# A depthwise convolution of the context tokens reads its taps from PSUM instead of from a padded copy in SBUF

## The chip, the cores and the metric

The kernel runs as one program on one core of a Trainium2 chip. Its time is the device time of one execution in microseconds, and the median over the runs is what counts. Besides that there is one profiled execution, whose instructions are all recorded; the rows below are from it. The engines are named as the profile names them: PE is TensorE (PEld its weight loads), DVE VectorE, ACT ScalarE, POOL GpSimd, and SP issues most DMAs.

## The reference, cut to what matters

One layer of a hybrid backbone: 512 latent tokens and 256 context tokens of 1024 channels. The context goes through the same input projection as the latents; its channels are convolved along the tokens, and only the final state of a scan over them is kept, as the start of the latent scans. Everything else (the latents' own convolution and scan, pooling, the output projection, a mixture of 32 experts) follows.

```python
def dwconv_centred(u, w, b):                       # 5 taps, 2 to each side, zeros beyond the ends
    y = lax.conv_general_dilated(u, w[:, None, :].astype(u.dtype), window_strides=(1,),
        padding=[(SSD_CONV // 2, SSD_CONV // 2)],
        dimension_numbers=("NWC", "WIO", "NWC"), feature_group_count=ch)
    return y + b.astype(u.dtype)
...
pc = hc @ w_in[l][:, :(XBCDT_COLS if last else IN_COLS)]
xbc_c = jax.nn.silu(dwconv_centred(pc[..., :CONV_CH], conv_w[l], conv_b[l]))
...
init_states = (ssd_final_state(xbc_c, dt_c, dt_bias[l], a_log[l], 0),
               ssd_final_state(xbc_c, dt_c, dt_bias[l], a_log[l], 1))
```

## The kernel before, in words

All data is fp32. A product is made of three matmuls of rounded halves: ACT writes the high part `hi` of a weight piece (L228), DVE or POOL the rest `lo` (L231), and PE multiplies hi by the high and low halves of the activations and lo by the high half.

The stage that the change touches is the loop over four head groups g at the end of the context's work. In each turn it issues, as written:

- for g = 0, 1 and 3 a block of the gate's projection (`z_block`, L353 to L355 on PE, ended by L369 on ACT and L370 on DVE);
- `ctx_conv(g)`: the group's four column blocks of 128 channels, two at a time (two halves, below called a and b). PE transposes them to channels on partitions (L447, into a PSUM bank of tag `S`, four such banks), ACT copies the bank to `xp` in SBUF (L452) between two zeroed columns on each side (POOL, L450 and L451), DVE applies the first tap and the bias (L456) and the other four taps (L459), each over all 256 tokens, ACT takes the tanh (L462), DVE completes the SiLU (L389), PE transposes back (L467), and ACT copies the result to `xc` (L468);
- `ctx_proj(g + 1)`: the next group's projection;
- `mod_row(g)`: one row of 1024 modulation values as a matrix-vector product outside PE: eight pieces of 512 KB are loaded into `mraw` (three buffers, L417 on SP's queue), the even ones are scaled by ACT (L419) and summed by POOL (L421), the odd ones are multiplied and summed by DVE (L423, L425), POOL adds both sums (L426), PE adds over the partitions (L432), DVE adds the bias (L434, for one row also L437), and the row is stored (L438, on ACT's queue) out of two more `mraw` buffers;
- `ctx_state(g)`: POOL scales `xc` (L407), PE makes the two states (L409), ACT copies them out (L477).

After the last group the memory of this stage is released, and the latents' groups start: their projections (`project`, L336 to L338) have their convolution taken straight from PSUM by `taps` (ACT L374 for the middle tap and the bias, DVE L378 for the four others). The first five of these projections (120 matmuls) need no memory of the context stage up to their convolution, so they run inside it.

A scheduler sets the order on each engine from its own estimate of the times: the program is written group by group, and it interleaves whatever it expects to be ready. The order is fixed when the program is built; on the chip each engine takes its list strictly in turn and waits on semaphores. SP's list is such a queue too: a load whose buffer isn't free holds up the loads behind it.

Of the kernel before, what the change touches and what calls it, by code (L numbers as in the profile page):

```python
# [5 lines left out]
F32 = mybir.dt.float32  # L6
# [4 lines left out]
AF = mybir.ActivationFunctionType  # L11
ALU = mybir.AluOpType
# [4 lines left out]
P = 128  # L17
# [3 lines left out]
TC = 256  # L21
# [76 lines left out]
def mixer_and_moe(tc, a):  # L98
    nc = tc.nc
    SC, VE, PO, PE, SP = nc.scalar, nc.vector, nc.gpsimd, nc.tensor, nc.sync  # L100
# [22 lines left out]
    def bank(tag):  # L123
        return psa.tile([P, T], F32, name="A", tag="A", bufs=4) if tag == "A" else \
            psb.tile([P, T], F32, name=tag, tag=tag, bufs=BUFS[tag])
# [83 lines left out]
    cw = pk.tile([P, 5, 20], F32, name="cw")  # L209
    cb = pk.tile([P, 20], F32, name="cb")  # L210
# [25 lines left out]
    for k in range(KT):  # L236
        for h in range(2):
# [7 lines left out]
            with tc.issue_after(wdma.ins):  # L245
                if 2 * k + h in (5, 9):
                    j = k // 2 - 1
# [41 lines left out]
    for j in range(16):  # L289
# [8 lines left out]
                            op0=ALU.add, op1=ALU.mult)  # L298
# [11 lines left out]
    for lo, n, which, oh_, ol_ in ((NT, NTC, 1, hch, hcl), (0, NT, 0, hxh, hxl)):  # L310
        for k in range(KT):
            tp = bank("S")
            w = n * P
            for j in range(n):
# [3 lines left out]
                             op0=ALU.mult, op1=ALU.add)  # L318
# [6 lines left out]
    pa = tc.alloc_tile_pool(name="pctx", bufs=1, side="left", reuse_waits="tile")  # L325
# [47 lines left out]
    def taps(ac, src, ct, n):  # L373
        SC.activation(ac, src, AF.Identity, scale=cw[:, 2, ct:ct + 1], bias=cb[:, ct:ct + 1])  # L374
        for j in (0, 1, 3, 4):
            o = j - 2
            u, v = max(0, -o), n - max(0, o)
            VE.scalar_tensor_tensor(ac[:, u:v], src[:, u + o:v + o], cw[:, j, ct:ct + 1], ac[:, u:v],  # L378
                                    op0=ALU.mult, op1=ALU.add)
# [8 lines left out]
    def silu_to(out, ac, tt):  # L388
        VE.scalar_tensor_tensor(out, tt, 1.0, ac, op0=ALU.add, op1=ALU.mult)  # L389
# [50 lines left out]
    def ctx_conv(g, ctxp):  # L440
        xc = pa.tile([P, NTC, T], F32, name="xc", bufs=2)
        for j2 in range(2):
            tp = bank("S")
            for i in range(2):
                j = 2 * j2 + i
                for c in range(NTC):
                    PE.transpose(tp[:, i * TC + c * P:i * TC + (c + 1) * P], ctxp[:, c, j * P:(j + 1) * P], ident)  # L447
            xp = pa.tile([P, 2, TC + 4], F32, name="xp2", bufs=2)
            ac = pa.tile([P, 2, TC], F32, name="ac2", bufs=2)
            PO.memset(xp[:, :, 0:2], 0.0)  # L450
            PO.memset(xp[:, :, TC + 2:], 0.0)  # L451
            SC.activation(xp[:, :, 2:2 + TC], tp.rearrange("p (i t) -> p i t", i=2), AF.Copy)  # L452
            for i in range(2):
                j = 2 * j2 + i
                ct = g * 3 + j if j < 3 else 12 + g
                VE.tensor_scalar(ac[:, i, :], xp[:, i, 0:TC], cw[:, 0, ct:ct + 1], cb[:, ct:ct + 1],  # L456
                                 op0=ALU.mult, op1=ALU.add)
                for q in range(1, 5):
                    VE.scalar_tensor_tensor(ac[:, i, :], xp[:, i, q:q + TC], cw[:, q, ct:ct + 1], ac[:, i, :],  # L459
                                            op0=ALU.mult, op1=ALU.add)  # L460
            tt = xp[:, :, 0:TC]
            SC.activation(tt, ac, AF.Tanh)  # L462
            silu_to(ac, ac, tt)
            tp = bank("S")
            for i in range(2):
                for c in range(NTC):
                    PE.transpose(tp[:, c * TC + i * P:c * TC + (i + 1) * P], ac[:, i, c * P:(c + 1) * P], ident)  # L467
            SC.activation(xc[:, :, j2 * TC:(j2 + 1) * TC], tp.rearrange("p (c t) -> p c t", c=NTC), AF.Copy)  # L468
        return xc
# [87 lines left out]
    for g in range(G):  # L557
        if g in ZP:
            z_block(ZP.index(g), pa, "tz")
        xcs[g] = ctx_conv(g, ctxps.pop(g))  # L560
        if g + 1 < G:
            ctxps[g + 1] = ctx_proj(g + 1)
        mod_row(g)
        init[g] = ctx_state(g, xcs.pop(g))
# [3 lines left out]
    pa = tc.alloc_tile_pool(name="pa", bufs=1, side="left", reuse_waits="tile")  # L568
# [216 lines left out]
    for i, ts in enumerate(cat):  # L785
        for j in range(3 + i):
            t = pcat.tile([P, 2, 4, 2 * P], F32R, name=f"cat{i}{j}", tag="raw", bufs=RC)
# [18 lines left out]
    for pr in range(2):  # L806
        cath, catl = cat[pr]
        for k2 in range(6):
            tp = bank("S")
# [5 lines left out]
            for i in range(2):  # L815
# [5 lines left out]
                                        op0=ALU.mult, op1=ALU.subtract)  # L821
# [1001 lines left out]
```

## Time and profile before

| | us |
|---|---|
| median of 3 runs | 1787.97 |
| lowest and highest of them | 1785.37 and 1789.52 |
| the profiled execution: device time | 1785.24 |
| its span, first to last instruction | 1783.4 |
| the context stage's conv part, first L447 to last L467 | 102.46 to 262.42 |
| the stream of the experts' weights | from about 480 to the end |

The device time of the profiled execution is 1.8 us longer than its span. In the rows below a time is counted from the span's start; "x4" is the number of instructions merged into a row, and the bracket at the end of a row says how long the engine was idle before it and what ended the idle time.

### The profile page before, as it was taken

How to read it: one execution, taken by the hardware profiler on the slowest of the kernel's cores; microseconds unless marked ns; L12 is line 12 of the kernel's file. 1: busy time of each engine (PE TensorE's matmuls, PEld its weight loads, DVE VectorE, ACT ScalarE, POOL GpSimd, SP SyncE). 2: the span in 40 equal slices, each digit the busy share in tenths (PEclk: the TensorE clock that was granted, in tenths of full speed). 3: DMA queues.
4: the chain of work that ended last, by engine and by line, in shares of the span. 5: the costliest groups of instructions: out<-in, count | busy, mean ns of one | idle time of the engine just before them, and what ended most of it. 6: DMA issues, size and time to landing. Idle time of an engine off the chain costs nothing. (4 is left out here: it accounts for less than half of the span.)

```text
span 1783.4 us, 21256 instructions
## 1 busy us (share of the span) xinstructions
PE 1634.9 (92%) x7311; PEld 1199.5 (67%) x7311; DVE 1524.0 (85%) x1486; ACT 1170.2 (66%) x1207; POOL 594.1 (33%) x287
## 2 busy tenths in 40 slices
PE   6999889998899899999999999999999998999995
PEld 2777667776777777767767667676666666666663
DVE  7767888987876989999989999966899999999994
ACT  6445336556643567787777877755678777787773
POOL 1213456779210102152040541502053454313302
PEclk9999899999999999999999999998999999999998
DMA  9646453323468789999999999985899999999973
GB/s 353 196 132 212 148 159 100 108 78 112 174 233 332 285 333 356 375 392 380 376 375 391 357 382 392 356 309 197 335 381 383 381 369 363 386 387 366 387 262 103
DMA packets 138417, 521.44 MB, mean 292 GB/s; under 512 B 14798, under 2 KB 44942, under 8 KB 106560
## 3 DMA queue, kind: packets, MB, share of 16 engines
q1 hardware_dynamic: 125446, 490.39, 72.4%
q0 software_dynamic: 6736, 16.70, 4.0%
q10 hardware_dynamic: 6122, 12.94, 2.2%
q8 instruction: 59, 0.97, 0.2%
q14 instruction: 54, 0.44, 0.1%
HBM read 508.26 MB, written 18.37 MB: 295 GB/s over the span
## 5 line engine op out<-in xcount | busy, mean ns | idle before, releaser
L1094 DVE TENSOR_TENSOR lo<-raw,hi 128x2048 fp32r<-128x2048 f32 x398 | 896.5, 2283 | 87.3 <-ACT hi L1093 83.3
L1093 ACT ACTIVATE hi<-raw 128x2048 fp32r<-128x2048 f32 x398 | 752.1, 1915 | 177.8 <-PE A L1357 111.0
L1382 POOL DMA_INDIRECT acc_scr<-y,ixi x32 | 216.7, 6773 | 544.8 <-DVE y L1380 444.6
L1357 PE MATMUL A<-lo,xh 128*128 128x512 f32 (+3 forms) x1072 | 315.4, 411 | 30.7 <-DVE lo L1094 26.7
L1357 PE MATMUL A<-hi,xh 128*128 128x512 f32 (+3 forms) x1072 | 308.9, 404 | 11.9 <-ACT hi L1093 8.0
L1357 PEld LDWEIGHTS A<-lo,xh 128*128 128x128 f32 (+3 forms) x1072 | 188.7, 185 | 117.7 <-DVE lo L1094 68.6
L1357 PEld LDWEIGHTS A<-hi,xh 128*128 128x128 f32 (+3 forms) x1072 | 194.7, 185 | 70.0 <-ACT hi L1093 10.6
L1117 POOL DMA_INDIRECT xg<-h_scr,ixi x30 | 113.1, 3771 | 256.5 <-PE S L1129 174.7
L1357 PE MATMUL S<-lo,ah 128*128 128x512 f32 (+3 forms) x512 | 163.9, 401 | 15.3 <-DVE lo L1094 15.2
L1357 PE MATMUL S<-hi,ah 128*128 128x512 f32 (+3 forms) x512 | 162.4, 398 | 1.7 <-DVE ah L1132 1.7
L1357 PE MATMUL A<-hi,xl 128*128 128x512 f32 (+3 forms) x544 | 154.5, 397 | 0.0
L1357 PEld LDWEIGHTS S<-lo,ah 128*128 128x128 f32 (+3 forms) x512 | 89.2, 181 | 50.3 <-DVE lo L1094 25.5
L1357 PEld LDWEIGHTS A<-hi,xl 128*128 128x128 f32 (+3 forms) x544 | 95.0, 175 | 31.7
L1357 PEld LDWEIGHTS S<-hi,ah 128*128 128x128 f32 (+3 forms) x512 | 91.1, 181 | 30.3 <-issue 3.1
L228 ACT ACTIVATE hi<-raw 128x1024 fp32r<-128x1024 f32 (+1 forms) x73 | 76.0, 1045 | 39.0 <-PE A L355 10.8
L231 DVE TENSOR_TENSOR lo<-raw,hi 128x1024 fp32r<-128x1024 f32 (+1 forms) x59 | 77.1, 1312 | 18.2 <-ACT hi L228 17.4
L1357 PE MATMUL S<-hi,al 128*128 128x512 f32 (+3 forms) x272 | 85.3, 394 | 0.0
L630 ACT ACTIVATE row<-row,nb 128x128 f32<-128x128 f32 x192 | 59.5, 389 | 37.1 <-POOL row L626 37.1
L336 PE MATMUL A<-hx,hi 128*128 128x512 f32 x160 | 66.2, 413 | 4.0 <-DVE at L378 2.5
L338 PE MATMUL A<-hx,lo 128*128 128x512 f32 x160 | 66.8, 417 | 0.0
L337 PE MATMUL A<-hx,hi 128*128 128x512 f32 x160 | 65.9, 412 | 0.0
L378 DVE SCALAR_TENSOR_TENSOR at<-A,cw,at 128x510 f32<-128x510 f32 (+1 forms) x80 | 57.8, 740 | 7.2 <-ACT at L374 6.6
(464 smaller groups left out, 2454.1 us busy)
## 6 DMA issues: line engine op xcount, KB each, us to landing
raw<-in_w_dram SPq DMA_DIRECT2D x384, 1024.0 KB
raw<-in_w_in_dram SPq DMA_DIRECT2D x36, 512.0 KB
mraw<-in_w_mod_dram SPq DMA_DIRECT2D x32, 512.0 KB
raw<-in_w_out_dram SPq DMA_DIRECT2D x14, 1024.0 KB
row<-cs_scr ACTq DMA_DIRECT2D x32, 384.0 KB
raw<-in_w_mod_dram SPq DMA_DIRECT2D x16, 512.0 KB
raw<-in_w_in_dram SPq DMA_DIRECT2D x16, 384.0 KB
xt<-in_x_dram SPq DMA_DIRECT2D x4, 512.0 KB
```

Of the source, the lines that this page charges most:

```text
L228: SC.activation(hi, r, AF.Copy)
L231: e.tensor_tensor(lo, r, hi.bitcast(F32), op=ALU.subtract)
L336: PE.matmul(lat, lhsT=hi[:, k, :], rhs=row_of(hxh, k), start=(k == 0), stop=False)
L337: PE.matmul(lat, lhsT=hi[:, k, :], rhs=row_of(hxl, k), start=False, stop=False)
L338: newest[0] = PE.matmul(lat, lhsT=lo[:, k, :], rhs=row_of(hxh, k), start=False, stop=(k == KT - 1))
L378: VE.scalar_tensor_tensor(ac[:, u:v], src[:, u + o:v + o], cw[:, j, ct:ct + 1], ac[:, u:v], op0=ALU.mult, op1=ALU.add)
L630: SC.activation(row[:, h, :], row[:, h, :], AF.Exp, bias=nb[:, c, i:i + 1])
L1093: ia = SC.activation(hi, r, AF.Copy)
L1094: i = VE.tensor_tensor(lo, r, hi.bitcast(F32), op=ALU.subtract)
L1117: PO.indirect_dma_start(out=t[0:m, :], out_offset=None, in_=h2_scr, in_offset=bass.IndirectOffsetOnAxis(ap=col[0:m, :], axis=0), bounds_ch ...
L1357: PE.matmul(bk[0:n, :], lhsT=u[:, k, 0:n], rhs=v[:, j * 512:(j + 1) * 512], start=(k == 0 and i == 0), stop=((last or m == LT and k == KT ...
L1382: PO.indirect_dma_start(out=acc_scr, out_offset=bass.IndirectOffsetOnAxis(ap=icol[0:m, :], axis=0), in_=y[0:m, :], in_offset=None, bounds_ ...
```

## The change

The copy to `xp`, its zeroed margins and the five taps over it go. The same `taps` function as for the latents takes their place, once for each column block: ACT writes the middle tap and the bias from PSUM to `ac`, and DVE adds the four others from PSUM, each over the tokens for which its neighbour exists (254 or 255 of 256). The tanh gets a tile `tt2` of its own, since it lay in `xp`.

```diff
-            xp = pa.tile([P, 2, TC + 4], F32, name="xp2", bufs=2)
             ac = pa.tile([P, 2, TC], F32, name="ac2", bufs=2)
-            PO.memset(xp[:, :, 0:2], 0.0)
-            PO.memset(xp[:, :, TC + 2:], 0.0)
-            SC.activation(xp[:, :, 2:2 + TC], tp.rearrange("p (i t) -> p i t", i=2), AF.Copy)
+            tt = pa.tile([P, 2, TC], F32, name="tt2", bufs=2)
             for i in range(2):
                 j = 2 * j2 + i
-                ct = g * 3 + j if j < 3 else 12 + g
-                VE.tensor_scalar(ac[:, i, :], xp[:, i, 0:TC], cw[:, 0, ct:ct + 1], cb[:, ct:ct + 1],
-                                 op0=ALU.mult, op1=ALU.add)
-                for q in range(1, 5):
-                    VE.scalar_tensor_tensor(ac[:, i, :], xp[:, i, q:q + TC], cw[:, q, ct:ct + 1], ac[:, i, :],
-                                            op0=ALU.mult, op1=ALU.add)
-            tt = xp[:, :, 0:TC]
+                taps(ac[:, i, :], tp[:, i * TC:(i + 1) * TC], g * 3 + j if j < 3 else 12 + g, TC)
             SC.activation(tt, ac, AF.Tanh)
             silu_to(ac, ac, tt)
```

From the edited place on, line numbers fall by 9 in the changed kernel: the transposes back are L458 there, the tanh L453, the copy to `xc` L459, the states' copies L468. L374 and L378 are then lines of both convolutions.

The scheduler makes another order of it on all engines, from the first context convolution to the end of the latents' scans. On PE the number of projection matmuls that stand between a half's transposes (L447) and its transposes back (L467, L458) changes so, counted along the two lists; both lists have 508 in all between the first L447 and the last transposes back:

| half | 0a | 0b | 1a | 1b | 2a | 2b | 3a | 3b |
|---|---|---|---|---|---|---|---|---|
| before | 63 | 49 | 62 | 55 | 53 | 59 | 66 | 45 |
| after | 64 | 59 | 74 | 54 | 72 | 79 | 35 | 0 |

The end of this part on PE, before; `ac_1753` is the result of half 3b, the rows up to it are projection matmuls of the latents' first group:

```order
L336 MATMUL A<-hx_94,hi 128x512
L337 MATMUL A<-hx_98,hi 128x512
L338 MATMUL A<-hx_94,lo 128x512
L467 MATMUL S<-con_76,ac_1753 128x128 x4
L432 MATMUL S<-macc,con_76 128x512 x2
L409 MATMUL S<-xd,xc 128x384 x3
```

The same place after; `ac_1706` is the result of half 3a and `ac_1731` that of half 3b:

```order
L338 MATMUL A<-hx_94,lo 128x512
L458 MATMUL S<-con_76,ac_1706 128x128 x4
L447 MATMUL S<-con_76,ctxp 128x128 x4
L458 MATMUL S<-con_76,ac_1731 128x128 x4
L432 MATMUL S<-macc,con_76 128x512 x2
L409 MATMUL S<-xd,xc 128x384 x3
```

No projection is left beside half 3b, and the transposes back of 3a have moved behind the last one.

On DVE, half 3a and the odd pieces of the last modulation row after the change; `ac_1706` as above, `macd` is that row's sum on DVE:

```order
L437 SCALAR_TENSOR_TENSOR mraw<-mraw 1x1024
L423 TENSOR_SCALAR macd<-mraw,sil 128x1024
L425 SCALAR_TENSOR_TENSOR macd<-mraw,sil,macd 128x1024
L378 SCALAR_TENSOR_TENSOR ac_1706<-S,cw,ac_1706 128x254
L378 SCALAR_TENSOR_TENSOR ac_1706<-S,cw,ac_1706 128x255
L231 TENSOR_TENSOR lo<-raw,hi 128x1024
L378 SCALAR_TENSOR_TENSOR ac_1706<-S,cw,ac_1706 128x255
L378 SCALAR_TENSOR_TENSOR ac_1706<-S,cw,ac_1706 128x254
L425 SCALAR_TENSOR_TENSOR macd<-mraw,sil,macd 128x1024
L378 SCALAR_TENSOR_TENSOR ac_1706<-S,cw,ac_1706 128x254
```

Before, at the same place, with `ac_1725` the result of half 3a and `at` that of a latent convolution:

```order
L456 TENSOR_SCALAR ac_1725<-xp_1724,cw,cb 128x256 x2
L378 SCALAR_TENSOR_TENSOR at<-A,cw,at 128x510
L459 SCALAR_TENSOR_TENSOR ac_1725<-xp_1724,cw,ac_1725 128x256 x3
L389 SCALAR_TENSOR_TENSOR at<-at 128x512
L459 SCALAR_TENSOR_TENSOR ac_1725<-xp_1724,cw,ac_1725 128x256 x2
L425 SCALAR_TENSOR_TENSOR macd<-mraw,sil,macd 128x1024
L459 SCALAR_TENSOR_TENSOR ac_1725<-xp_1724,cw,ac_1725 128x256 x2
L378 SCALAR_TENSOR_TENSOR at<-A,cw,at 128x510
L459 SCALAR_TENSOR_TENSOR ac_1725<-xp_1724,cw,ac_1725 128x256
L425 SCALAR_TENSOR_TENSOR macd<-mraw,sil,macd 128x1024
```

The latents' taps that stood in turn with half 3a have moved ahead of L437; the half's taps now stand in turn with the row's pieces alone, and behind one more of them.

On ACT the same place after, with the semaphores that an instruction waits for in brackets:

```order
L374 ACTIVATE ac_1706<-S,cb,cw 128x256 [waits PE_49]
L228 ACTIVATE hi<-raw 128x1024 [waits PE_49,Pool_49]
L419 ACTIVATE mraw<-mraw,sil 128x1024 [waits DMAHW2_49,DMAHW7_49,DVE_49,Activation_49]
L468 ACTIVATE init_1562<-S 128x384 [waits PE_49]
L374 ACTIVATE ac_1706<-S,cb,cw 128x256 [waits DVE_49]
L419 ACTIVATE mraw<-mraw,sil 128x1024 [waits DMAHW1_49,Pool_49]
L228 ACTIVATE hi<-raw 128x1024 [waits PE_49]
L453 ACTIVATE tt_1707<-ac_1706 128x512 [waits DVE_49,Activation_49]
```

The second block's L374 waits for DVE, and that is the last tap of the first block; the tanh stands behind two loads' pieces (L419).

## Rows read from the trace of the kernel before

**Rows 1.** The page: busy time and share of the span by engine, instructions.

```profile
PE 1634.9 (92%) x7311; PEld 1199.5 (67%) x7311; DVE 1524.0 (85%) x1486; ACT 1170.2 (66%) x1207; POOL 594.1 (33%) x287
```

**Rows 2.** Busy time in stretches (context stage, experts): stretch, us, engines, granted clock, DMA share, GB/s.

```profile
102.40:262.40 160.00, 144.16 (x605) 113.48 (x604) 127.89 (x157) 68.68 (x91) 57.75 (x42) 0.94 0.53 165
600.00:800.00 200.00, 190.41 (x842) 145.29 (x843) 185.20 (x181) 144.98 (x106) 44.73 (x11) 0.98 0.96 363
```

**Rows 3.** PE in order of time: start us, us, instruction, idle before and its releaser.

```profile
102.46 0.60 PE L447 MATMUL S<-con,ctxp 128*128 128x128 f32 x4
...
150.21 0.80 PE L354 MATMUL A<-lo,hch 128*128 128x512 f32 x1 [3.67 <-DVE lo L231]
...
198.94 1.09 PE L467 MATMUL S<-con,ac 128*128 128x128 f32 x4 [4.88 <-DVE ac L389]
...
202.42 0.79 PE L336 MATMUL A<-hx,hi 128*128 128x512 f32 x1 [1.54 <-DVE yt L370]
...
218.72 1.88 PE L432 MATMUL S<-macc,con 128*128 128x512 f32 x4
...
239.72 0.39 PE L337 MATMUL A<-hx,hi 128*128 128x512 f32 x1
...
243.35 0.39 PE L338 MATMUL A<-hx,lo 128*128 128x512 f32 x1
...
247.22 0.63 PE L467 MATMUL S<-con,ac 128*128 128x128 f32 x4 [3.48 <-DVE ac L389]
...
262.42 0.63 PE L467 MATMUL S<-con,ac 128*128 128x128 f32 x4 [2.28 <-DVE ac L389]
```

**Rows 4.** The 5 us behind the idle time before 150.21, columns as in rows 2.

```profile
150.00:155.00 5.00, 4.79 (x11) 3.80 (x12) 5.00 (x5) 2.46 (x4) 4.06 (x1) 0.50 0.64 193
```

**Rows 5.** Single lines: count, ns shortest/median/longest, first and last start.

```profile
L456 DVE TENSOR_SCALAR ac<-xp,cw,cb x16: 400/410/2486, 103.8 to 257.0; 128x256 f32<-128x256 f32 x16
L459 DVE SCALAR_TENSOR_TENSOR ac<-xp,cw,ac x64: 471/474/2657, 104.5 to 260.1; 128x256 f32<-128x256 f32 x64
L378 DVE SCALAR_TENSOR_TENSOR at<-A,cw,at x80: 730/737/751, 212.6 to 405.5; 128x510 f32<-128x510 f32 x40, 128x511 f32<-128x511 f32 x40
L820 DVE SCALAR_TENSOR_TENSOR cat<-S,pv,cat x24: 466/473/484, 468.2 to 495.7; 128x256 fp32r<-128x256 f32 x24
L452 ACT ACTIVATE xp<-S x8: 579/597/613, 103.1 to 253.3; 128x512 f32<-128x512 f32 x8
L819 ACT ACTIVATE cat<-S,pv x24: 450/473/499, 467.7 to 493.4; 128x256 fp32r<-128x256 f32 x24
L462 ACT ACTIVATE xp<-ac x8: 618/630/634, 110.9 to 260.6; 128x512 f32<-128x512 f32 x8
L389 DVE SCALAR_TENSOR_TENSOR ac<-xp,ac x8: 674/680/692, 112.2 to 261.6; 128x512 f32<-128x512 f32 x8
```

**Rows 6.** Groups by line in 102.4 to 262.4: busy us, mean ns, idle before.

```profile
L459 DVE SCALAR_TENSOR_TENSOR ac<-xp,cw,ac 128x256 f32<-128x256 f32 x64 | 35.2, 609 | 0.0
L456 DVE TENSOR_SCALAR ac<-xp,cw,cb 128x256 f32<-128x256 f32 x16 | 15.0, 976 | 1.5 <-ACT xp L452 1.5
```

**Rows 7.** DVE and POOL in order of time.

```profile
119.70 3.25 DVE L459 SCALAR_TENSOR_TENSOR ac<-xp,cw,ac 128x256 f32<-128x256 f32 x8
...
184.95 3.38 POOL L231 TENSOR_TENSOR lo<-raw,hi 128x1024 fp32r<-128x1024 f32 x1
...
186.00 2.48 DVE L456 TENSOR_SCALAR ac<-xp,cw,cb 128x256 f32<-128x256 f32 x1
```

**Rows 8.** Modulation rows 2 and 3: DVE's and ACT's pieces in order of time.

```profile
178.09 0.75 DVE L423 TENSOR_SCALAR macd<-mraw,sil 128x1024 f32<-128x1024 f32 x1 [3.52 <-DMA mraw<-in_w_mod_dram]
...
182.66 3.41 DVE L425 SCALAR_TENSOR_TENSOR macd<-mraw,sil,macd 128x1024 f32<-128x1024 f32 x1 [2.03 <-DMA mraw<-in_w_mod_dram]
...
191.58 1.16 ACT L419 ACTIVATE mraw<-mraw,sil 128x1024 f32<-128x1024 f32 x1 [5.35 <-DMA mraw<-in_w_mod_dram]
...
229.78 0.75 DVE L423 TENSOR_SCALAR macd<-mraw,sil 128x1024 f32<-128x1024 f32 x1 [1.30 <-DMA mraw<-in_w_mod_dram]
```

## The prediction

> **What bounds the kernel now.** The page first: PE is busy for 92% of the span, DVE for 85% [rows 1]. Then the stretches: where the experts' weights stream, the DMA engines are busy for 0.96 and PE for 95% [rows 2]; that part is paced by its own load stream, none of its instructions is edited, and so it starts earlier or later by what the stages ahead of it gain or lose. The part in question, from the first context transposes at 102.46 us to the last transposes back at 262.42 us [rows 3], has DMA at 0.53 and PE at 144 of 160 us: it is PE's, with holes. PE in order of time shows five: 3.67 us for a `lo` of DVE, 4.88, 3.48 and 2.28 us for a SiLU of the context convolution, 1.54 us for a gate row of DVE [rows 3], together 15.85 us. [...] Without both the same matmuls would take 160.0 - 15.85 - 9.6 = 134.5 us.
>
> **Why DVE is late there.** A tap takes 474 ns in the middle of the list but 609 in the mean and up to 2657; L456 410, but 976 in the mean [rows 5, 6]. The long ones lie beside a POOL instruction: L456 at 186.00 took 2.48 us while POOL's `lo` ran from 184.95 to 188.33 [rows 7]. The taps of the latents, which read PSUM, never needed more than 751 ns in 80 [rows 5], though POOL works beside them as well.
>
> **The change part by part.**
> DVE: 16 L456 and 64 L459 go, 15.0 + 35.2 = 50.2 us [rows 6]. 64 taps from PSUM come. No such row exists at 255 elements; L820 is the same operation from PSUM at 256 elements and took 473 ns, and half of L378's 737 is the bound from below, 369 ns; from above a whole L378, 737 [rows 5]. I take 473: 30.3 us, 19.9 us less (bounds 3 to 27), nearly half of it the stretching beside POOL, 64 x (609 - 474) = 8.6 and 16 x (976 - 410) = 9.1 us. DVE is busy for 128 of these 160 us [rows 2], so what this gives PE is what its holes were worth, not the 20 us.
> ACT: 8 copies of 597 ns go, 16 L374 of 256 elements come; L819, from PSUM with a scale, took 473 [rows 5]: +2.8 us on an engine that is busy for 69 of 160 us [rows 2]. Its idle time hides that; without it, it would cost the 2.8.
> POOL: 16 memsets of four elements go, with their waits for the last user of `xp`; the modulation rows' sums stood behind them. POOL is busy for 58 of these 160 us [rows 2]: I count nothing, with a microsecond either way.
> One half alone: before, transposes, copy 0.6, ten DVE instructions at a pitch of some 0.4 (eight took 3.25 [rows 7]), tanh 0.63, SiLU 0.68. After, ACT 0.47, four taps 1.7, ACT 0.47, four taps 1.7, tanh, SiLU, with some 0.1 us at each of six hand-overs and 0.6 for the transposes: 6.8 us. The order shows why it isn't shorter: the second block's L374 waits for DVE's last tap of the first, so both blocks stand in turn, with ACT's queue in between.
> In rows alone, ACT and DVE could work on one bank's two halves at once and a half would take 6.3 us. [...] I go by the order, which has the wait.
> [...] Here L820 from PSUM and L459 from SBUF differ by 1 ns [rows 5], and the trace decides.
>
> **What is moved.** The list of PE before spends 45 matmuls beside half 3b; after, the halves 0b to 2b take more and 3a has 35, 3b none. PE has nothing left to do while 3b runs, and little in 3a. So I compute when the last transposes back start, the event at 262.42 before, in three steps. Let Z be the start of the sum over partitions (L432) of modulation row 2, 218.72 before [rows 3].
> First Z. From Z to the last transposes back PE has, after the change, 57 matmuls at 0.227 (3.63 us for 16 [rows 3]), that is 12.9 us, 1.9 for L432, three blocks of transposes at 0.6 [rows 3], and for four L409, each one matmul of 384 columns where L432 is two of 512, 4 x 0.94 x 384 / 512 = 2.8: 19.4, and since such durations overlap a little, 19 us. At full clock and without holes Z would be at 102.46 + 134.5 - 19 = 218. With no mercy it keeps the 10.1 us of holes that lay before Z, and 7 of the 9.6 of clock: 235. The three holes stand behind DVE's stretched conv work or (1.54) at its heels, and the new lists give the halves 1a, 2a and 2b 12 to 20 matmuls more. I take one hole of 1.5 and 2 of clock: Z = 221.5.
> Then half 3a. Its tanh stands on ACT behind pieces 4 and 6 of modulation row 3, its taps on DVE in between pieces 3 and 5, so it is tied to these loads. Row 3's first DVE piece came at 229.78, 11.1 us behind Z; in row 2 the sixth piece came 13.5 us behind the first (191.58 - 178.09), waiting for its DMA [rows 8]. So piece 6 is at Z + 24.6; its scaling 1.16 [rows 8], one `hi` of the same size 1.1, tanh 0.63, SiLU 0.68 and hand-overs make Z + 28.3 for 3a's transposes back. PE ran dry 18 to 19 us behind Z; it waits some 10.
> Then half 3b with nothing beside it: 6.8 us, and 0.4 because a last piece (L425) stands ahead of its taps: Z + 35.5 = 257.0, which is 5.4 us earlier than 262.42. The bounds for this span: 28, if 3a is not held by the loads (done by Z + 20, and 8), and 43.7, that of before, if the pieces come as late as they did then.
> Last, the restart: behind holes of 10 and 7 us PE runs at 0.50 for some 5 us as in [rows 4], which is spent on L432, L409 and the first matmuls: +3.5 us (0, if they wait for POOL anyhow, to 5). What follows, the latents' scans, gets another order as well with the same instructions; I count 0, with 3 us either way.
> Sum: -5.4 + 3.5 = -1.9 us. Made on the profiled execution, whose device time is its span and 1.8 us around it: 1785.24 - 1.9 = 1783.3. That execution was 2.7 us faster than the median of its kernel's runs, 1787.97, so on the median: **1786.1 us**. The forecast is no change, that is within 0.2% or 3.6 us, which is what a measurement of this kernel can tell from none.
>
> **The rivals.**
> First rival, faster: the loads don't bind half 3a. For it: without the latents' taps in between, DVE takes pieces 3 and 5 as soon as they land, and the sixth piece of row 2, whose pace I use, came late behind a DVE piece stretched to 3.41 us [rows 8]. Then the span is 28 instead of 35.5 and the restart 2.5 instead of 3.5: -1.9 - 8.5 = -10.4, so 1777.6. Against it: SP issues row 3's pieces only when row 2's result has left its buffers, and L437 stays ahead of that.
> Second rival, slower: the cover is spent without a gain. Place: DVE in modulation row 1 (half 1a) and row 2. With the `lo` and the modulation row's pieces still read from SBUF on DVE, POOL's sums stretch those instead of the taps, PE waits as before, and Z stays near 231 (holes 8 us, clock 5). Then 231 + 35.5 + 3.5 = 270 against 262.42: +7.6, so 1795.6. It decides from Z = 227 on (227 + 39 = 266, which is +3.6). For it: the hole before 150.21 was a late `lo`, not a tap [rows 3]. Against it: DVE has 20 us less to do.
> That the change does not do what it says is no rival: the copies, the memsets and the first tap are gone from the lists, and the taps read PSUM.
>
> **How the numbers follow.** No change 0.36; first rival and smaller gains of its kind (over 3.6 us faster) 0.36; second rival and its kind 0.28. The two errors that matter are Z (218 to 235) and the span to the last transposes back (28 to 43.7); each is some 4 to 5 us wide on either side of what I take, and the scans add 3, so about 7 us together: 8 in 10 lie within 9 us, 1777 to 1796. The no-change case alone is 1783 to 1791.
>
> **What would show it.** In the profile after: no hole of PE ahead of a transposes back of groups 1 and 2; DVE's taps of 256 elements near 473 ns with none over 600; two holes of PE before the last two transposes back (L458), some 10 and 7 us, the first ended by a SiLU whose tanh waited behind L419 for a load; the granted clock near 0.5 behind them; the last of these transposes at 255 to 261 us; everything behind shifted by about as much. The prediction is wrong if these two holes together are under 8 us (faster), if PE's holes in groups 1 and 2 stay above 6 us (slower), or if the scans from 270 to 470 us change by more than 4 us.

## The result, and the profile after

The changed kernel takes **1799.13 us** in the median of six runs (1796.62 to 1804.34), the kernel before, on the same chip, 1786.74 (1783.86 to 1789.52): 1.0078 times as long, 95% interval 1.0065 to 1.0091. It is slower, by 12.4 us between the medians and some 14 us by the ratio, where no change was forecast. Its profiled execution took 1797.39 us, with a span of 1795.6, 12.2 longer than that of before. One run of version M below took 2261.86 us at a granted clock of 0.65, where its other five show 0.96, and is left out of M's median.

The page of the changed kernel, its engines as in [rows 1]:

```profile
PE 1638.5 (91%) x7311; PEld 1201.6 (67%) x7311; DVE 1508.5 (84%) x1470; ACT 1175.0 (65%) x1215; POOL 588.7 (33%) x271
```

DVE has 15.5 us less to do and POOL 5.4, and the program is longer. ACT has 4.8 us more, and PE is busy 3.6 us longer with the same 7311 matmuls; both are far less than 12.2, so most of the time went into waiting. The stretches tell where. The changed kernel, columns as in [rows 2]; the first stretch is the context stage, from its first L447 to the last transposes back (L458), the next two are the latents' scans:

```profile
102.80:257.90 155.10, 137.12 (x606) 108.68 (x604) 114.69 (x141) 73.22 (x99) 57.58 (x30) 0.96 0.56 177
270.00:380.00 110.00, 108.22 (x503) 84.48 (x502) 95.51 (x129) 67.27 (x165) 82.74 (x77) 0.99 0.29 90
380.00:470.00 90.00, 72.79 (x330) 56.38 (x329) 57.69 (x80) 44.98 (x122) 59.87 (x56) 0.87 0.25 85
```

The same two stretches of the scans in the kernel before:

```profile
270.00:380.00 110.00, 102.83 (x486) 80.41 (x487) 98.47 (x130) 67.43 (x165) 80.39 (x74) 1.00 0.30 99
380.00:470.00 90.00, 78.77 (x415) 61.44 (x414) 72.01 (x120) 53.42 (x142) 68.72 (x64) 0.98 0.27 87
```

The context stage is shorter (155.1 us where [rows 2] has 160). Up to 380 us the changed kernel is ahead: 503 matmuls against 486. From 380 to 470 us it does 330 against 415; every engine does less, and the granted clock is 0.87 instead of 0.98. So the loss lies here, 120 us behind the edited code, in instructions that the change does not touch.

PE in the context stage of the changed kernel, columns as in [rows 3]:

```profile
102.77 0.60 PE L447 MATMUL S<-con,ctxp 128*128 128x128 f32 x4
...
156.30 0.50 PE L354 MATMUL A<-lo,hch 128*128 128x512 f32 x1 [1.77 <-DVE lo L231]
...
191.81 0.50 PE L336 MATMUL A<-hx,hi 128*128 128x512 f32 x1 [2.22 <-DVE yt L370]
...
223.93 1.88 PE L432 MATMUL S<-macc,con 128*128 128x512 f32 x4
...
248.50 1.12 PE L458 MATMUL S<-con,ac 128*128 128x128 f32 x4 [6.60 <-DVE ac L389]
...
257.86 1.12 PE L458 MATMUL S<-con,ac 128*128 128x128 f32 x4 [7.39 <-DVE ac L389]
```

No transposes back wait in groups 1 and 2 any more; the two holes have moved to the last two, where PE has nothing else. The event that ended this part at 262.42 [rows 3] is at 257.86.

The scans have a landmark that is easy to follow: each of the 16 (four groups, four chunks of 128 tokens) has one run of 12 small matmuls on PE. The 1st, the 8th (end of group 1) and the 16th of the kernel before, by the same columns:

```profile
294.20 1.45 PE L643 MATMUL S<-xh,row 128*128 128x64 f32 x12
...
386.37 1.45 PE L643 MATMUL S<-xh,row 128*128 128x64 f32 x12
...
463.80 1.55 PE L643 MATMUL S<-xh,row 128*128 128x64 f32 x12
```

The same of the changed kernel, and the 13th between, which waited:

```profile
290.72 1.45 PE L634 MATMUL S<-xh,row 128*128 128x64 f32 x12
...
381.15 1.45 PE L634 MATMUL S<-xh,row 128*128 128x64 f32 x12
...
435.35 2.79 PE L634 MATMUL S<-xh,row 128*128 128x64 f32 x12 [4.46 <-DVE row L627]
...
476.94 1.55 PE L634 MATMUL S<-xh,row 128*128 128x64 f32 x12
```

The changed kernel is 3.5 us ahead at the 1st scan, 5.2 ahead at the 8th and 13.1 behind at the 16th: groups 2 and 3 take 95.8 us instead of 77.4. Between these two marks both kernels do the same work (before, then changed, columns as in [rows 2]):

```profile
386.37:463.80 77.43, 69.10 (x361) 53.61 (x360) 61.86 (x92) 45.38 (x122) 59.98 (x57) 0.98 0.30 99
...
381.15:476.94 95.79, 77.77 (x363) 60.15 (x361) 62.16 (x91) 44.97 (x122) 59.27 (x57) 0.88 0.24 80
```

Of the 18.4 us, 9.7 are idle time of PE (18.0 us instead of 8.3), and 8.7 are as many matmuls at a lower granted clock, 0.88 instead of 0.98. They come in several steps: 3.9 us up to the 10th scan, 5.1 more at the 11th, 2.2 up to the 13th, 6.7 at the 14th and 0.5 behind it. From the 16th scan to the end of the span both take the same time (1318.7 us changed, 1319.6 before).

What the engines wait for there, in the changed kernel (POOL, ACT and DVE in order of time; L617 masks a row, L228 and L231 make a weight's two halves, L626 and L627 are a scan's mask sum and product):

```profile
419.75 0.86 POOL L617 TENSOR_SCALAR_AFFINE_SELECT row<-row 128x768 f32<-128x768 f32 x1 [4.55 <-DMA row<-cs_scr]
...
429.77 2.52 DVE L626 TENSOR_TENSOR row<-row 128x768 f32<-128x768 f32 x1
...
432.22 2.01 DVE L231 TENSOR_TENSOR lo<-raw,hi 128x1024 fp32r<-128x1024 f32 x1
...
434.15 0.94 DVE L627 TENSOR_TENSOR row<-row,S 128x768 f32<-128x768 f32 x1
...
438.40 1.06 ACT L228 ACTIVATE hi<-raw 128x1024 fp32r<-128x1024 f32 x1 [9.71 <-DMA raw<-in_w_out_dram]
```

These are heads of queues. ACT stands still for 9.71 us in front of a weight piece whose load has not landed, with the exponentials of the next scan and the issue of the next rows' loads behind it. The 13th scan's product (L627) stands on DVE behind a `lo` that it does not need. In the kernel before, the same piece's `hi` stands behind half of those exponentials and waited 0.33 us.

The rows' loads (`cs_scr`), which ACT's queue issues, are late as well: from the 8th to the 16th scan POOL's masks wait for them for 15.7 us in seven places, and in the kernel before for 3.6 us in four.

### The profile page after: what moved, and what is told of

Read it like the earlier page. It is cut to its first block, busy times and chain, and to the rows that moved or that the text cites. A ratio compares the mean times of both kernels' runs of the same rounds, so it can differ in the third digit from the quotient of the medians.

```text
span 1795.6 us, 21236 instructions
## 1 busy us (share of the span) xinstructions
PE 1638.5 (91%) x7311; PEld 1201.6 (67%) x7311; DVE 1508.5 (84%) x1470; ACT 1175.0 (65%) x1215; POOL 588.7 (33%) x271
## 5 line engine op out<-in xcount | busy, mean ns | idle before, releaser
L1085 DVE TENSOR_TENSOR lo<-raw,hi 128x2048 fp32r<-128x2048 f32 x398 | 896.6, 2283 | 88.8 <-ACT hi L1084 84.2
L1348 PEld LDWEIGHTS S<-hi,ah 128*128 128x128 f32 (+3 forms) x512 | 91.0, 181 | 30.3 <-issue 3.1
L228 ACT ACTIVATE hi<-raw 128x1024 fp32r<-128x1024 f32 (+1 forms) x73 | 76.2, 1047 | 43.1 <-PE A L355 16.3
L231 DVE TENSOR_TENSOR lo<-raw,hi 128x1024 fp32r<-128x1024 f32 (+1 forms) x59 | 82.8, 1405 | 20.1 <-ACT hi L228 17.1
L378 DVE SCALAR_TENSOR_TENSOR at<-A,cw,at 128x510 f32<-128x510 f32 (+1 forms) x80 | 58.2, 741 | 5.1 <-ACT at L374 4.3
```

What stands on the lines that cost most here:

```text
L228: SC.activation(hi, r, AF.Copy)
L231: e.tensor_tensor(lo, r, hi.bitcast(F32), op=ALU.subtract)
L1085: i = VE.tensor_tensor(lo, r, hi.bitcast(F32), op=ALU.subtract)
L1348: PE.matmul(bk[0:n, :], lhsT=u[:, k, 0:n], rhs=v[:, j * 512:(j + 1) * 512], start=(k == 0 and i == 0), stop=((last or m == LT and k == KT ...
```

## The experiments

The scheduler makes one list per engine when the program is built. The scan stage has the same 1664 instructions in both kernels, in the same program order, and the load queue's list is the same; the lists of ACT, DVE, POOL and PE differ in 787 places. "Old order" and "new order" are the lists of the kernel before and of the changed one. An order is set by hand with edges that only fix the place in an engine's own queue and wait for nothing:

```diff
+    scan_from = len(nc.cur_bb.bb.instructions)
     POOL_EVERY[0] = PEV
     start_group(0)
...
+    traced = nc.cur_bb.bb.instructions[scan_from:]
+    for order in scan_order():
+        for i, j in zip(order[1:], order):
+            tc.add_manual_dep(traced[i], traced[j].name, mybir.DependencyInfo(
+                mybir.DependencyClass.NoSync, mybir.DependencyReason.DATA), reason="order of the scans")
     pa.release()
     pk.release()
```

`scan_order()` returns one list of indices per engine. All runs together (the "third `hi`" is the high half of the third piece of the output projection's weights, for whose load ACT stood still for 9.71 us; "row 3" is the last modulation row); the ratio is to the kernel before on the same chip, the scans' times are starts in the profiled execution:

| | convolution | order of the scans | median us | ratio, 95% interval | 1st | 8th | 16th scan | 8th to 16th |
|---|---|---|---|---|---|---|---|---|
| before | old | old | 1786.74 | 1 | 294.20 | 386.37 | 463.80 | 77.4 |
| after | new | new | 1799.13 | 1.0078 (1.0065 to 1.0091) | 290.72 | 381.15 | 476.94 | 95.8 |
| A | new | old | 1786.34 | 0.9994 (0.9978 to 1.0009) | 296.71 | 387.31 | 465.65 | 78.3 |
| B | old | new | 1804.07 | 1.0095 (1.0075 to 1.0114) | 296.12 | 387.04 | 481.77 | 94.7 |
| C | new | new, old from group 2 on | 1787.67 | 1.0005 (0.9995 to 1.0015) | 292.22 | 386.52 | 464.75 | 78.2 |
| D | new | new, old in the last part | 1793.12 | 1.0031 (1.0018 to 1.0044) | 290.16 | 383.05 | 470.00 | 87.0 |
| E | new | old, new in the last part | 1798.86 | 1.0064 (1.0049 to 1.0079) | 295.64 | 385.79 | 476.35 | 90.6 |
| F | new | new, third `hi` later | 1798.72 | 1.0069 (1.0045 to 1.0093) | 292.67 | 385.62 | 475.85 | 90.2 |
| G | old | old, third `hi` earlier | 1794.01 | 1.0041 (1.0027 to 1.0056) | 297.68 | 389.88 | 474.05 | 84.2 |
| H | new | new, third piece's own buffer | 1798.63 | 1.0071 (1.0058 to 1.0084) | 291.20 | 382.82 | 474.54 | 91.7 |
| I | new | as H, one `lo` later | 1801.48 | 1.0086 (1.0072 to 1.0100) | 292.71 | 383.17 | 477.79 | 94.6 |
| J | new | new, ACT old from group 2 on | 1816.35 | 1.0163 (1.0150 to 1.0177) | 292.03 | 390.18 | 493.36 | 103.2 |
| K | new | new, PE old from group 2 on | 1801.32 | 1.0079 (1.0065 to 1.0093) | 290.28 | 382.75 | 474.75 | 92.0 |
| L | new | all old from group 2 on but PE | 1805.91 | 1.0100 (1.0085 to 1.0116) | 289.97 | 392.18 | 482.48 | 90.3 |
| M | copy kept | almost new | 1811.77 | 1.0148 (1.0127 to 1.0168) | 302.79 | 393.58 | 489.68 | 96.1 |
| N | new | old, row 3 later | 1787.31 | 1.0008 (0.9993 to 1.0023) | 296.00 | 386.08 | 463.75 | 77.7 |
| O | new | as C, row 3 later | 1787.78 | 1.0012 (1.0002 to 1.0022) | 292.83 | 385.58 | 464.42 | 78.8 |

**A and B: the order or the convolution.**

> The changed convolution, but the instructions of the latents' scan stage (1664 of them) stand on ACT, DVE, POOL and PE in the order that they had before. Theory A (the loss is the new order of the scans): the gain of the context stage stays, 3.5 us at 270 us, and the scans cost what they cost before, so about 1786.7 - 3.5 = 1783 us (1780 to 1787). Theory B (the loss comes from what the new convolution itself leaves behind, such as the clock or the place of the loads, and the order only follows): it stays at 1797 to 1800.

> The convolution of before, but the scan stage in the order of the changed kernel. Theory A: the scans lose their 13 to 16 us here too and the gain of 3.5 us is missing, so 1799 to 1806. Theory B: the order costs nothing by itself, 1785 to 1789.

Run A, the last two transposes back, the 13th and the 16th scan on PE:

```profile
248.78 1.11 PE L512 MATMUL S<-con,ac 128*128 128x128 f32 x4 [5.10 <-DVE ac L443]
...
262.16 1.11 PE L512 MATMUL S<-con,ac 128*128 128x128 f32 x4 [11.41 <-DVE ac L443]
...
431.18 1.45 PE L688 MATMUL S<-xh,row 128*128 128x64 f32 x12
...
465.65 1.55 PE L688 MATMUL S<-xh,row 128*128 128x64 f32 x12
```

Its scans from 380 to 470 us, by stretch:

```profile
380.00:470.00 90.00, 80.38 (x420) 62.09 (x418) 70.66 (x111) 53.10 (x142) 68.82 (x65) 0.98 0.26 85
```

Run B, the 13th and the 16th scan:

```profile
439.43 2.79 PE L697 MATMUL S<-xh,row 128*128 128x64 f32 x12 [4.56 <-DVE row L690]
...
481.77 1.55 PE L697 MATMUL S<-xh,row 128*128 128x64 f32 x12
```

And its stretch:

```profile
380.00:470.00 90.00, 72.44 (x327) 55.65 (x327) 57.63 (x79) 47.56 (x130) 64.79 (x62) 0.87 0.25 85
```

The order decides, in both directions. With the old order the changed convolution has 420 matmuls from 380 to 470 us at a clock of 0.98 and no wait before the 13th scan; with the new order the old convolution has 327 at 0.87 and the same wait of 4.6 us. From the 8th to the 16th scan the two orders take 77.4 and 78.3, or 95.8 and 94.7 us, whichever convolution stands before them. The end times are 1786 and 1799 to 1804. Theory A is shown. One of its numbers was wrong: the changed convolution did not keep its 3.5 us in run A. The hole before the last half is 11.41 us there, with no projection beside that half and two pieces of modulation row 3 (L479, 3.22 and 3.40 us) ahead of its taps on DVE:

```profile
249.24 3.22 DVE L479 SCALAR_TENSOR_TENSOR macd<-mraw,sil,macd 128x1024 f32<-128x1024 f32 x1 [0.52 <-DMA mraw<-in_w_mod_dram]
...
252.63 3.40 DVE L479 SCALAR_TENSOR_TENSOR macd<-mraw,sil,macd 128x1024 f32<-128x1024 f32 x1 [0.17 <-DMA mraw<-in_w_mod_dram]
```

The late rows' loads go with the order too: POOL's masks wait for them for 3.6 us in run A and 14.0 in run B, from the 8th to the 16th scan.

**C, D, E: where.**

> The changed kernel with its own order of the scans up to group 3, and the order of before for what follows among itself (scans of group 3, pooled heads, first pieces of the output projection). If the loss lies in this last part (the wait of ACT for the third piece's load, 9.71 us, and DVE's lo of the second piece ahead of the mask product of scan (3,0), behind which PE waited 4.47 us): 8 to 12 us are won, 1787 to 1791. If it lies earlier, in groups 1 and 2: 1795 to 1799.

> The counterpart: the changed convolution with the order of before up to group 3 and in the places of the last part, but the last part's instructions among themselves in the order of the changed kernel. If the loss lies in the last part: 1786.3 + 8 to 12 = 1794 to 1798. If it lies earlier: 1785 to 1789.

> The changed convolution; the instructions of the scan stage up to the end of group 1's scans keep the order of the changed kernel among themselves, those from group 2 on the order of before among themselves. The changed kernel reached its 8th scan at 381.15 us, the one before at 386.37; from the 8th to the 16th the one before took 77.4 us, the changed one 95.8. If the loss lies only from group 2 on, both good parts add up: 1787 - 5 = 1782 (1779 to 1785), faster than both. If the good start and the good end exclude each other: 1785 to 1793.

The old order from group 2 on is enough: C is back at 1787.67, so the loss lies behind the 8th scan. The good start of the new order is not kept beside it: C is 2.0 us ahead at the 1st scan and 0.2 behind at the 8th; from the 7th to the 8th, where the two lists meet, it takes 20.6 us, the changed kernel 14.7. The last part alone (group 3's scans, the pooled heads, the first output weights) costs 12.5 us in the old order's surroundings (A to E) and gives 6 back in the new one's (after to D), so its own order matters and what stands around it as well. D lies between the two forecasts made for it, so neither place alone holds the loss.

**F, G, H, I: is it one instruction?**

> The changed kernel with one instruction moved: ACT's hi half of the third piece of the output projection's weights stands behind the copy of the first pooled head, not ahead of the exponentials of scan (3,1). Theory A1 (inside theory A, the loss is mostly this one head-of-line wait, 9.71 us of idle ACT at 428.69): 6 to 9 us are won, 1790 to 1793, and ACT has no gap over 5 us there. Theory A2 (the wait only moves on, since POOL, DVE and the load are late as well, and the loss is spread over many places): 1796 to 1800.

> The kernel before with the same instruction moved the other way: the third piece's hi half ahead of the exponentials of scan (3,1) and of the pooled heads' copies. Theory A1: ACT stands still until that load lands, near 437 us, and 4 to 8 us are lost, 1791 to 1795. Theory A2: 1786 to 1789.

> The changed kernel with all of its orders as they are, but the third piece of the output projection's weights is loaded into the second buffer of xh, which is free since scan (2,3), instead of a raw buffer that the lo of an earlier piece frees at 434 us. If ACT's 9.71 us of idle time at 428.69 is its queue standing behind this one late load: the load lands some 5 us earlier, ACT's gap falls under 5 us and 3 to 6 us are won, 1793 to 1796. If the work behind it is late anyhow: 1797 to 1801.

> As the run in which the third piece has a buffer of its own, and one more place undone: DVE's lo of the second piece stands behind the mask product, the o2 product and the gate of scan (3,0), as it does in the kernel before, not ahead of them; all else is in the order of the changed kernel. In that run PE stood idle for 4.46 us until this mask product, which stood behind a mask sum of 2.52 us and the lo of 2.01 us. If the loss is made of such places, one by one: PE's hole falls to about 2.5 us and the time to 1794 to 1797. If the work behind is late anyhow: 1797 to 1801.

The edit of F (the lines that note the two instructions are left out); G has the edge the other way round, from the twelve exponentials of scan (3,1) and the heads' copies to this `hi`:

```diff
...
                 hi, lo = split_weights(r, [P, D])
+                if (pr, kk) == (0, ks[2]):
+                    tc.add_manual_dep(hi_act[0].ins, pt_act[0].ins.name, mybir.DependencyInfo(
+                        mybir.DependencyClass.NoSync, mybir.DependencyReason.DATA), reason="the first pooled head goes ahead")
```

H's lists are those of the changed kernel; in I the index of one `lo` stands three places later in DVE's list. F and G hold no list by hand: behind their edge the scheduler moved instructions of ACT, DVE and PE as well, so only H and I undo a place with all else in its order.

The edit of H:

```diff
-                r = raw_tile([P, D])
+                if (pr, kk) == (0, ks[2]):
+                    r = pa.tile([P, NT, GW], F32, name="xh", bufs=2).rearrange("p c w -> p (c w)")[:, 0:D]
+                else:
+                    r = raw_tile([P, D])
```

Run H, the same `hi` on ACT and the 13th scan on PE:

```profile
434.41 1.06 ACT L282 ACTIVATE hi<-xh 128x1024 fp32r<-128x1024 f32 x1 [4.04 <-DMA xh<-in_w_out_dram]
...
437.02 2.80 PE L688 MATMUL S<-xh,row 128*128 128x64 f32 x12 [4.46 <-DVE row L681]
```

Run I, the 13th scan:

```profile
435.60 2.79 PE L688 MATMUL S<-xh,row 128*128 128x64 f32 x12 [2.66 <-DVE row L681]
...
447.89 0.74 PE L784 MATMUL A<-hi,cath 128*128 128x512 f32 x2 [3.64 <-DVE cath L738]
```

Each wait fell as it should: ACT's from 9.71 to 4.04 us (H), PE's from 4.46 to 2.66 (I). The time did not follow: 1798.63 and 1801.48. In I the next late thing came through: PE waits 3.64 us at 447.89, where it waited 0.33 in the changed kernel. H, with edges that spell out the changed kernel's own lists, takes the changed kernel's time, so the edges by themselves cost nothing to speak of. Moving the instruction later (F) did not help either. In the kernel before, moving it forward (G) cost 7 us, the time that theory A1 forecast, though other instructions moved with it. Theory A1 falls for the changed kernel; for G it fits, and is not shown.

**J, K, L: whose queue?**

> The changed kernel with its own order on DVE, POOL and PE, and on ACT the order of before from group 2 on. Theory Q (ACT's queue is what loses: it issues the loads of the rows and its exponentials stand behind instructions that wait): 1788 to 1792. Theory P (PE's list loses, which puts more matmuls of the next group ahead of a scan's own): 1797 to 1801. Theory J (the lists lose only together, each engine waits for the latest of the four): 1795 to 1800 here and in the next.

> The changed kernel with its own order on ACT, DVE and POOL, and on PE the order of before from group 2 on. Theory Q: 1797 to 1801. Theory P: 1788 to 1792. Theory J: 1795 to 1800.

> The changed kernel with its own order on PE alone, and on ACT, DVE and POOL the order of before from group 2 on (with PE's too it took 1787.7). Theory Q: 1787 to 1791. Theory P: 1796 to 1801. Theory J: between, 1790 to 1796.

Neither ACT's queue nor PE's alone: with ACT's old list beside the others' new ones the kernel is the slowest of all, and PE's old list gives nothing back. All old lists but PE's are still slower than all new ones. DVE's and POOL's lists alone were not tried. Run J, PE behind group 3:

```profile
459.63 1.22 PE L783 MATMUL A<-hi,cath 128*128 128x512 f32 x2 [8.60 <-DVE sst L852]
```

Run L, ACT:

```profile
426.54 1.86 ACT L683 ACTIVATE row<-row,nb 128x128 f32<-128x128 f32 x6 [10.62 <-PE S L471]
```

Where lists of two origins meet, each engine comes to an instruction whose input another engine has put off: PE waits 8.60 us in J, ACT 10.62 in L. Theories Q and P fall. Theory J, that the lists lose only together, is the nearest, but it forecast 1795 to 1800 for runs J and K and 1790 to 1796 for run L; run J is 16 us above that and run L 10. What is shown is that lists of two plans, mixed by engine, took 1801 to 1816 us here, no less than the worse plan; why is argued from such waits.

**M: is PSUM as the taps' source at fault?**

> The changed kernel, but ACT copies the transposed channels to SBUF first and the taps read this copy (still without margins and memsets, the middle tap on ACT); the order of the scans is then nearly that of the changed kernel (its PE list is the same). If the order sets the time and the source of the taps little: 1799 to 1805, the taps on DVE stretched again. If reading PSUM is itself at fault: back at 1785 to 1790.

```diff
-            tt = pa.tile([P, 2, TC], F32, name="tt2", bufs=2)
+            xp = pa.tile([P, 2, TC], F32, name="xp2", bufs=2)
+            SC.activation(xp, tp.rearrange("p (i t) -> p i t", i=2), AF.Copy)
+            tt = xp
...
-                taps(ac[:, i, :], tp[:, i * TC:(i + 1) * TC], g * 3 + j if j < 3 else 12 + g, TC)
+                taps(ac[:, i, :], xp[:, i, :], g * 3 + j if j < 3 else 12 + g, TC)
```

Run M, the taps of the context on DVE (count, ns shortest/median/longest), columns as in [rows 5]:

```profile
L378 DVE SCALAR_TENSOR_TENSOR ac<-xp,cw,ac x64: 470/476/2632, 105.6 to 267.6; 128x254 f32<-128x254 f32 x32, 128x255 f32<-128x255 f32 x32
```

The same taps in M by shape, columns as in [rows 6]:

```profile
L378 DVE SCALAR_TENSOR_TENSOR ac<-xp,cw,ac 128x255 f32<-128x255 f32 x32 | 24.3, 807 | 0.0
L378 DVE SCALAR_TENSOR_TENSOR ac<-xp,cw,ac 128x254 f32<-128x254 f32 x32 | 22.5, 729 | 4.6 <-ACT ac L374 4.6
```

And its last half on PE, from the first projection beside it to the transposes back:

```profile
258.62 0.78 PE L337 MATMUL A<-hx,hi 128*128 128x512 f32 x1
...
262.94 0.39 PE L338 MATMUL A<-hx,lo 128*128 128x512 f32 x1
...
269.66 1.09 PE L460 MATMUL S<-con,ac 128*128 128x128 f32 x4 [6.34 <-DVE ac L389]
```

Going back to SBUF did not give the time back: the context stage ends 11.8 us later (269.66 against 257.86) and the program 12.6, which is slower than expected. M's taps go up to 2632 ns again, and the 64 take 46.8 us of DVE instead of 30.7; in the kernel before, all nine taps over 600 ns (L456 and L459) overlap a POOL instruction. But M is not the changed kernel with another source alone. PE's list is the same in the scans only; in the context stage the scheduler planned anew, with 14 projections beside the last half (258.62 to 262.94) where the changed kernel has none. So the 16 us of DVE can come from the source and from what POOL did beside it, and how much of the 12.6 us is due to them and how much to the order is open. That PSUM as a source is not what lost the time is shown by run A, which reads it and takes 1786.34.

**N, O: the holes ahead of the last two halves.**

> The changed convolution with the scans in the order of before, and the DVE pieces of modulation row 3 queued behind the taps of the last context halves (pieces 1 and 3 behind half 3a, 5 and 7 behind 3b), so that the taps don't stand behind a piece that waits for its load. If the two holes of PE there (5.1 and 11.4 us with this order) are the taps waiting behind the pieces, the last transposes back come at 253 to 256 instead of 262 and the time is 1776 to 1782. If the latents then wait for the buffers of the later row, nothing is won: 1784 to 1789.

> As the one with the order of before from group 2 on, and the DVE pieces of modulation row 3 behind the taps of the last two context halves. With whole orders of before these edges brought the last transposes back 3.5 us forward and the end nothing; here the latents' first scans follow the context stage more closely, so if PE's hole ahead of the last half is what they wait for, 2 to 4 us less than the kernel without the edges; otherwise the same within 2.

```diff
...
+            if q == 3 and k % 2:
+                tc.add_manual_dep(x.ins, last_tap[k // 4].ins.name, mybir.DependencyInfo(
+                    mybir.DependencyClass.NoSync, mybir.DependencyReason.DATA), reason="the convolution goes ahead")
```

Run N, the last two transposes back on PE:

```profile
249.50 1.11 PE L518 MATMUL S<-con,ac 128*128 128x128 f32 x4 [4.71 <-DVE ac L444]
...
258.66 1.11 PE L518 MATMUL S<-con,ac 128*128 128x128 f32 x4 [7.19 <-DVE ac L444]
```

With the pieces behind the taps the last hole falls from 11.41 to 7.19 us, so the taps did stand behind the pieces; half 3a's hole stays at 4.71, so that half is not held by DVE's pieces. The end does not move (1787.31; O 1787.78): the 16th scan comes at 463.75 as in the kernel before. Neither version beats the kernel before.

## Why the prediction was wrong

The step that failed is its last term: "What follows, the latents' scans, gets another order as well with the same instructions; I count 0, with 3 us either way." Measured, this term is 16.6 us: the changed kernel is 3.5 us ahead at the 1st scan and 13.1 behind at the 16th. The order was known to differ, but counting "the same instructions" took the order for neutral. The prediction named the sign to look for (the scans change by more than 4 us), and that is what happened; it gave it no chance of its own.

The terms before it, one by one:

- **DVE's taps**, taken as 473 ns with none over 600. The changed kernel, columns as in [rows 5]:

```profile
L378 DVE SCALAR_TENSOR_TENSOR ac<-S,cw,ac x64: 468/482/485, 104.0 to 255.9; 128x254 f32<-128x254 f32 x32, 128x255 f32<-128x255 f32 x32
...
L374 ACT ACTIVATE ac<-S,cb,cw x16: 546/558/566, 103.4 to 253.7; 128x256 f32<-128x256 f32 x16
```

  Right: 485 ns at most in 64, where the old taps went up to 2657 [rows 5], and 30.7 us in all (forecast 30.3). Yet DVE's busy time fell by 15.5 us and not by 19.9, since some of the stretching moved to what still reads SBUF, as the second rival had it: one SiLU (L389) of the context, from 200.90 us on, took 2.88 us beside POOL's L426 (199.97 to 203.23), where none had taken over 692 ns [rows 5], and a piece 3.37 (below). In run M, with the same instruction on a copy in SBUF, the taps take 2632 ns at most and 16.1 us more of DVE in all. In the median they differ little: 482 ns from PSUM against 476 from SBUF.
- **ACT's middle tap** was mis-sized: 558 ns instead of 473, 1.4 us in 16, beside idle time.
- **Z**, the sum of modulation row 2, was forecast at 221.5 and came at 223.93; the holes before it are 1.77 + 2.22 = 3.99 us instead of 1.5. No run shows the 9.6 us of clock in its sum: it is an estimate, 0.06 x 160 us from [rows 2], and by the same arithmetic the changed kernel, at a granted clock of 0.96 over 155.1 us, has 6.2. The second rival's point (Z over 227) was not reached; its time, 1795.6, is nearer to the result than the forecast, but by another mechanism.
- **Half 3a** was forecast at Z + 28.3 and came at Z + 24.6 (248.50). Row 3's piece 6 on ACT (the first row below) was earlier than row 2's pace made it:

```profile
244.26 1.15 ACT L419 ACTIVATE mraw<-mraw,sil 128x1024 f32<-128x1024 f32 x1 [1.36 <-DMA mraw<-in_w_mod_dram]
...
246.72 0.63 ACT L453 ACTIVATE tt<-ac 128x512 f32<-128x512 f32 x1 [0.37 <-DVE ac L378]
...
248.37 3.37 DVE L425 SCALAR_TENSOR_TENSOR macd<-mraw,sil,macd 128x1024 f32<-128x1024 f32 x1
```

  That is Z + 20.3, not Z + 24.6. The tanh was then released by DVE's last tap, not by the load.
- **Half 3b** took 9.4 us instead of 7.2, because the piece ahead of its taps (the last row above) was stretched to 3.37 us, beside POOL's L231 (247.85 to 250.65). That the last transposes back come at 257.86, with 257.0 forecast, is luck: the errors of the three steps, +2.4, -3.7 and +2.2 us, cancel.
- **The restart**, 3.5 us: the first L432 behind the hole took 3.62 us instead of 1.88, at a granted clock of 0.50. The gain over before is 4.6 us at the last transposes back and still 3.5 at the 1st scan, so the restart and what lies between cost 1.1 us, and the sum without the scans, 1.9, was too small.

So the local part came out near its forecast, a small gain at the context stage's end, with terms that were each some 2 to 4 us off. With the scans in the old order (run A) the changed kernel takes 1786.34 us, and 1786.1 was predicted; that they agree so closely is luck, since the context stage of run A ends at 262.16 and not at 257.0.

What stays open: why the new order is slow as a whole. It is shown that the four lists together lose 13 us with the new convolution and 17 with the old, that they do so behind the 8th scan, and that engines then wait at the heads of their queues for instructions that another engine does late. It is not shown that any one place or queue carries the loss: three edits of single places (F, H, I) and three by engine (J, K, L) gave nothing back. One rival stands: the rows' loads on ACT's queue come late with the new order (POOL waits for them for 15.7 us after and 14.0 in B, and with the old order for 3.6, before and in A). No run moved these issues alone, and ACT's own waits for the masks hardly differ (21.0 us after, 19.0 before). Whether the scheduler's estimate of some duration is what misleads it was not tried either.

## What to carry to other kernels

Where a scheduler sets the order, a local edit is also a new order for everything that it schedules together with it. Compare the lists far behind the edit, look for instructions that moved ahead of others in the queues of waiting engines (a weight's `hi` ahead of the exponentials), and give the new order a price and a chance of both signs: here it outweighed the edit several times over. To judge the edit itself, time it with the old order held by edges that wait for nothing; an edit that leaves the order to the scheduler, as M did, measures both at once. Don't mix lists of two plans, and don't take the longest wait for the cause before one edit has shown it.

## What the runs showed of the hardware

An instruction of DVE that adds a scaled tap from SBUF took 474 ns in the median and up to 2657 [rows 5]; all four of its 64 over 600 ns (L459, before) overlap a POOL instruction. The same from PSUM took at most 485 ns, 3 over its median of 482 (after), though 23 of the 64 overlap one. ACT's scaled and biased copy of 256 elements took 558 ns from PSUM, 85 more than the scaled copy without a bias [rows 5]. From the 8th to the 16th scan, with the same work, the granted clock is 0.88 with the new order (after) and 0.98 with the old (before), and PE is idle there for 18.0 us (after) and 8.3 (before). From 380 to 470 us the clock is 0.98 with the old order in run A as well, and 0.87 with the new one in run B. Behind a wait PE lost time in matmuls too: the 12 small ones at 435.35, behind a hole of 4.46 us, took 2.79 us at a granted clock of 0.50, where those at 381.15 took 1.45 at 1.00 (after).
